# The first modulation of a hybrid encoder layer: weight blocks stationary, two or four columns of c moving

## The chip, the cores and the metric

The kernel runs on one NeuronCore of a Trainium2 chip. The core has TensorE (PE in the profile; its weight loads are listed apart as PEld), VectorE (DVE), ScalarE (ACT), GpSimd (POOL) and SyncE (SP), which here only issues transfers, and 16 DMA engines. The metric is the device time of one execution in microseconds, as the median of several. The chip can grant TensorE less than its full clock; the profile lists the granted clock (1.00 is full).

## The reference

One encoder layer for 512 prompt frames and 64 sample frames, with D = 2048. What matters here is its first step: a vector c per request (one for the prompt, one for the sample) goes through SiLU and a matrix of 2048 x 12288, which gives six modulation vectors; the first two shift and scale the normalised input before the big input projection.

```
mod = jax.nn.silu(c) @ w_ada[l] + b_ada[l]
sh1, sc1, g1, sh2, sc2, g2 = jnp.split(mod[:, None, :], N_MOD, axis=-1)
h = rmsnorm(x, norm1[l]) * (1 + sc1) + sh1
mix, s_a, s_b, s_c = token_mixers(h, ...)      # begins with proj = h @ w_in
x = x + g1 * mix
h = rmsnorm(x, norm2[l]) * (1 + sc2) + sh2
f, s_f = conv_ffn(h, ...)
x = x + g2 * f
```

All inputs and outputs are float32.

## The kernel before

After the opening stage (`head`) come the head recurrences with the rest of the input projection, the output projection, the up projection with its convolution, and the down projection. All large products are made from float32r parts: a float32 operand is split into a rounded high part and a remainder (`split`: ScalarE makes `wh`, L649; VectorE makes `wl` as the difference, L650), and three products of parts replace one float32 product (`mm6`, L561 and L563).

`head` computes the vectors sh1 and sc1 (indices 0 and 1 of `mod`) in four groups g of 512 columns. `modulation(g)` does for each group two halves, first the scale (mi = 1), then the shift (mi = 0). A half reads eight weight tiles from `w_ada`, each of 256 rows by 512 columns in 512 KB, as two blocks of 128 rows (k). Six of the eight are split into `wh` and `wl`. The other two (k0 = 4 and 12) stay whole in float32; over the eight halves these are sixteen tiles. The tiles land in `hraw` (5 buffers) or `raw` (3 buffers); split parts have three buffers each.

On TensorE the columns of c are the stationary operand and the weights move, 512 columns at a time, into one PSUM bank. For split tiles the stationary operand is `cst[:, k]` with NW = 66 columns, of which four hold something (the high parts and the remainders of the two vectors) and the rest are zeros written by GpSimd; there are four such matmuls per tile (L757, L758). For whole tiles it is `cs4[:, k]` with four columns, two of them zeros, in float32 (L753, two per tile). The result lies in four PSUM rows, 512 columns wide. It is brought onto the partitions in three steps: VectorE copies it to `rw` (L760), four small matmuls of `rw` against a selection matrix add high part and remainder and turn it (L763, into a second bank `pc`), and VectorE adds the bias b_ada into `mod` (`put_mod`, L797). After both halves `scale_mod` (L803) makes the scale `s1`.

With group 0's modulation the input x is loaded, transposed on TensorE (L698) and its row sums made (L725, L726); the vectors (biases, gains) are loaded and transposed (L623, L624). From there on the order is: modulation(g + 1), then for the four k of group g the split of the modulated x (`split_mod`, L583, L584, L586: `tmp`, `hh`, `hl`), the narrow columns (L877) and two blocks of the projection (L561, L563; the groups of the profile with `fh`, `fl`). What is called here "products" are those 256 matmuls of 288 moving columns.

A scheduler decides the order on each engine from the order of the code and priorities: loads and splits of weight tiles are issued with a raised priority (`high_priority`), so they stand some instructions earlier than in the code. Each engine works through its own queue in that order.

The same helper pattern appears later, in `ada_block` (L820, L826): there the other four modulation vectors are made by VectorE, and sixteen matmul instructions per block (L826: `acc`, 128 x 128, stationary, one column of ones moving) sum them over partitions.

Of the kernel before, what the change touches and what calls it, by code (L numbers as in the profile page):

```python
# [8 lines left out]
F32 = mybir.dt.float32  # L9
F32R = mybir.dt.float32r  # L10
I32 = mybir.dt.int32
AF = mybir.ActivationFunctionType
ALU = mybir.AluOpType
# [3 lines left out]
P = 128  # L17
D = 2048
KD = 16
# [28 lines left out]
NW = 66  # L48
# [53 lines left out]
class Kern:  # L102
# [554 lines left out]
    def head(self, pool):  # L657
        nc, i = self.nc, self.i
        V, A, T = nc.vector, nc.scalar, nc.tensor
# [2 lines left out]
            next(vectors)  # L662

        self.ct = self.cp.tile([P, 2, KD], F32, name="ct")
        cst = pool.tile([P, KD, NW], F32R, tag="cst", bufs=1, name="cst")
        nc.gpsimd.memset(cst.bitcast(F32), 0.0)
        for s in range(2):
            A.activation(self.ct[:, s], self.vmap[f"c{s}"], AF.Silu)
        cs4 = pool.tile([P, KD, 4], F32, tag="cs4", bufs=1, name="cs4")
        nc.gpsimd.memset(cs4, 0.0)  # L670
        for s in range(2):
            V.tensor_copy(cs4[:, :, s], self.ct[:, s])
            A.activation(cst[:, :, s], self.ct[:, s], AF.Copy)
            V.tensor_tensor(cst[:, :, 2 + s], self.ct[:, s], cst[:, :, s].bitcast(F32), op=ALU.subtract)
        self.mod = self.cp.tile([P, 6, KD, 2], F32, name="mod")
# [61 lines left out]
        def hraw():  # L737
            if next(turns) == "r":
                return self.raw()
            return pool.tile([P, 1024], F32, tag="hraw", bufs=5, name=self.name("hraw"))  # L740

        def modulation(g, between=lambda: None):
            for mi in (1, 0):
                ps = self.bank()
                c0 = mi * D + g * 512
                for k0 in range(0, KD, 2):
                    between()
                    src = i["w_ada"][0, k0 * P:(k0 + 2) * P, c0:c0 + 512].rearrange("(k p) n -> p k n", p=P)
                    if k0 in (4, 12):
                        raw = hraw().rearrange("p (k n) -> p k n", k=2)  # L750
                        nc.sync.dma_start(raw, src)
                        for k in range(2):
                            T.matmul(ps[:4], cs4[:, k0 + k], raw[:, k], start=False, stop=False)  # L753
                        continue
                    wh, wl = self.wtile(src, hraw())
                    for k in range(2):
                        T.matmul(ps[:NW], cst[:, k0 + k], wh[:, k], start=(k0 + k == 0), stop=False)  # L757
                        T.matmul(ps[:NW], cst[:, k0 + k], wl[:, k], start=False, stop=(k0 + k == KD - 1))  # L758
                rw = pool.tile([4, 512], F32, tag="rw", bufs=1, name=self.name("rw"))
                V.tensor_copy(rw, ps[:4])  # L760
                pc = self.bank()
                for j in range(4):
                    T.matmul(pc[:, 2 * j:2 * j + 2], rw[:, j * P:(j + 1) * P], self.c["sel"][:4, 16:18], start=True, stop=True)  # L763
                self.put_mod(mi, 4 * g, pc)
                for _ in vectors:
                    pass
            self.scale_mod(s1, 1, "norm1", 4 * g)

        plan = [[] for _ in range(16)]
        for b in range(5):  # L770
            for f, at in ((x_load, 0), (x_turn, X_LAG), (x_norm, X_LAG + 1)):
                plan[X_AT[b] + at].append(lambda f=f, b=b: f(b))
        step = iter(plan)
        modulation(0, lambda: [f() for f in next(step)])
        rx = x_rows()
        self.ps_nar, self.ps_q0 = self.pgt(), self.pgt()
        for g in range(4):
            if g < 3:
                modulation(g + 1)
            ks = range(4 * g, 4 * g + 4)  # L780
            nar = self.narrow_w(pool, 4 * g)
            qw, kw = [self.split(pool, self.w_in(off)(4 * g, 4 * g + 4), "f", 512, 3) for off in (OFF_BQ, OFF_BK)]
            for k in ks:
                hh, hl = self.htiles(k)
                tmp = pool.tile([P, 2, HT], F32, tag="tmp", bufs=2, name=self.name("tmp"))
                self.split_mod(xT[:, k], rx, s1[:, k], self.mod[:, 0, k], hh, hl, tmp)
                nc.sync.dma_start(self.xs[k], xT[:, k])
                self.h.append((hh, hl))
                self.mm_narrow(k, nar[:, k % 4])
                for ps, w in ((self.ps_q0, qw), (ps_k0, kw)):  # L790
                    self.mm6(ps, w[0][:, k % 4], w[1][:, k % 4], self.h[k], k == 0, k == KD - 1)
        raw = self.xr()
        self.ps_k0 = raw[:, :2 * HT].rearrange("p (h t) -> p h t", h=2)
        V.tensor_copy(self.ps_k0, ps_k0[:, :, :HT])

    def put_mod(self, mi, k0, pc):
        self.nc.vector.tensor_tensor(  # L797
            self.mod[:, mi, k0:k0 + 4], pc[:, :8].rearrange("p (j s) -> p j s", s=2),
            self.vec("b_ada", mi * KD + k0, 4).unsqueeze(2).to_broadcast([P, 4, 2]), op=ALU.add)

    def scale_mod(self, out, mi, norm, k0, n=4):

# [1188 lines left out]
```

## Time and profile before

| | |
|---|---|
| Median of 3 runs | 2870.66 us (2866.38 to 2871.43) |
| The profiled execution | 2869.18 us |
| Its span, first to last instruction | 2867.4 us |
| Mean granted TensorE clock | 0.992 |
| PE busy | 2810.4 us (98%), 20596 matmul instructions |
| PEld busy | 2708.7 us (94%) |
| DVE busy | 2301.9 us (80%) |
| ACT busy | 1355.0 us (47%) |
| POOL busy | 320.6 us (11%) |
| HBM read, written | 356.24 MB, 40.13 MB |

In the page's rows a group reads: line, engine, operation, result <- operands (buffer numbers left out), for a matmul the stationary block as rows*columns and the result, the count, then busy time, mean duration in ns, and the idle time of the engine just before with what ended it. Matmuls overlap and their ends are modelled, so the time between two starts in the timeline says more of their cost than their durations. Times in the timeline and the windows are us from the span's start. The opening stage takes the first 160 us.

### The profile page before, as it was taken

How to read it: one execution, taken by the hardware profiler on the slowest of the kernel's cores; microseconds unless marked ns; L12 is line 12 of the kernel's file. 1: busy time of each engine (PE TensorE's matmuls, PEld its weight loads, DVE VectorE, ACT ScalarE, POOL GpSimd, SP SyncE). 2: the span in 40 equal slices, each digit the busy share in tenths (PEclk: the TensorE clock that was granted, in tenths of full speed). 3: DMA queues.
4: the chain of work that ended last, by engine and by line, in shares of the span. 5: the costliest groups of instructions: out<-in, count | busy, mean ns of one | idle time of the engine just before them, and what ended most of it. 6: DMA issues, size and time to landing. Idle time of an engine off the chain costs nothing.

```text
span 2867.4 us, 52042 instructions
## 1 busy us (share of the span) xinstructions
PE 2810.4 (98%) x20596; PEld 2708.7 (94%) x20596; DVE 2301.9 (80%) x3742; ACT 1355.0 (47%) x2379; POOL 320.6 (11%) x587
## 2 busy tenths in 40 slices
PE   7999999999999999999999999999999999999998
PEld 3599999999999999999999999999999999999997
DVE  5788878777778777468888888888887889999995
ACT  7574566544333333255444444444444464434453
POOL 0005432224310001001000000000000000000000
PEclk9999999999999999999999999999999999999999
DMA  9975555545455448433333333333333343443451
GB/s 308 306 209 148 157 149 161 158 140 152 129 166 172 146 131 251 123 119 102 102 101 102 108 106 108 102 108 108 101 101 105 105 150 114 123 127 118 126 169 67
DMA packets 522441, 399.80 MB, mean 139 GB/s; under 512 B 50793, under 2 KB 453956, under 8 KB 522196
## 3 DMA queue, kind: packets, MB, share of 16 engines
q1 hardware_dynamic: 516772, 385.79, 45.3%
q0 software_dynamic: 5424, 10.68, 1.2%
q8 instruction: 162, 2.65, 0.4%
q14 instruction: 83, 0.68, 0.1%
HBM read 356.24 MB, written 40.13 MB: 138 GB/s over the span
## 4 chain that ended last, share of the span: by engine, by line
PE 82%; DVE 9%; DMA 3%; ACT 3%; issue 2%; SPq 0%; POOL 0%; ACTq 0%; DVEq 0%
PE g L561 19%; PE g L563 10%; PE g L1373 9%; PE g L1374 8%; PE g L1375 8%; PE bank L1374 3%; PE bank L1373 3%; PE bank L1375 3%; DVE wl L1558 2%; PE g L1606 2%; PE g L1608 2%; PE g L1607 2%; DMA raw<-in_w_down_dram 1%; PE bank L162 1%; PE bank L826 1%
## 5 line engine op out<-in xcount | busy, mean ns | idle before, releaser
L1373 PE MATMUL g<-slot,wh 128*128 128x290 f32 x1760 | 534.2, 304 | 2.4 <-ACT p L1385 2.4
L1374 PE MATMUL g<-slot,wh 128*128 128x290 f32 x1760 | 526.6, 299 | 0.0
L1375 PE MATMUL g<-slot,wl 128*128 128x290 f32 x1760 | 520.9, 296 | 0.0
L561 PE MATMUL g<-hh,wh 128*128 128x288 f32 x1984 | 450.4, 307 | 2.4 <-ACT hh L1160 1.3
L561 PE MATMUL g<-hl,wh 128*128 128x288 f32 x1984 | 432.3, 298 | 0.0
L563 PE MATMUL g<-hh,wl 128*128 128x288 f32 x1984 | 432.0, 298 | 0.0
L1320 ACT ACTIVATE wh<-raw 128x1024 fp32r<-128x1024 f32 x176 | 186.8, 1061 | 393.1 <-PE g L1374 376.8
L1373 PEld LDWEIGHTS g<-slot,wh 128*128 128x128 f32 x1760 | 331.8, 189 | 16.9 <-ACT p L1385 11.3
L1375 PEld LDWEIGHTS g<-slot,wl 128*128 128x128 f32 x1760 | 337.2, 192 | 0.0
L1374 PEld LDWEIGHTS g<-slot,wh 128*128 128x128 f32 x1760 | 335.6, 191 | 0.1
L561 PEld LDWEIGHTS g<-hh,wh 128*128 128x128 f32 x1984 | 319.1, 190 | 5.6 <-ACT hh L1160 1.5
L561 PEld LDWEIGHTS g<-hl,wh 128*128 128x128 f32 x1984 | 321.3, 189 | 0.3
L563 PEld LDWEIGHTS g<-hh,wl 128*128 128x128 f32 x1984 | 319.6, 189 | 0.2 <-issue 0.2
L649 ACT ACTIVATE wh<-raw 128x1024 fp32r<-128x1024 f32 x163 | 172.6, 1059 | 309.1 <-PE g L561 272.6
L650 DVE TENSOR_TENSOR wl<-raw,wh 128x1024 fp32r<-128x1024 f32 x163 | 199.1, 1222 | 52.8 <-ACT wh L649 50.9
L820 DVE SCALAR_TENSOR_TENSOR acc<-xr,ct,acc 128x512 f32<-128x512 f32 x322 | 230.4, 751 | 1.5 <-DMA xr<-in_w_ada_dram 1.5
L1321 DVE TENSOR_TENSOR wl<-raw,wh 128x1024 fp32r<-128x1024 f32 x176 | 214.8, 1220 | 19.3 <-ACT wh L1320 19.2
L1606 PE MATMUL g<-slot,wh 128*128 128x288 f32 x760 | 224.8, 296 | 2.3 <-DVE slot L1623 1.1
L1608 PE MATMUL g<-slot,wl 128*128 128x288 f32 x760 | 224.4, 296 | 0.3 <-DVE wl L1558 0.3
L1607 PE MATMUL g<-slot,wh 128*128 128x288 f32 x760 | 224.4, 295 | 0.0
L1374 PE MATMUL bank<-slot,wh 128*128 128x290 f32 x704 | 210.3, 299 | 0.0
L1373 PE MATMUL bank<-slot,wh 128*128 128x290 f32 x704 | 209.6, 298 | 0.0
(416 smaller groups left out, 6083.0 us busy)
## 6 DMA issues: line engine op xcount, KB each, us to landing
raw<-in_w_up_dram SPq DMA_DIRECT2D x176, 512.0 KB, 4.0
raw<-in_w_in_dram SPq DMA_DIRECT2D x108, 512.0 KB, 3.9
xr<-in_w_ada_dram SPq DMA_DIRECT2D x86, 512.0 KB, 3.9
raw<-in_w_down_dram SPq DMA_DIRECT2D x76, 512.0 KB, 3.6
ax<-in_w_ada_dram SPq DMA_DIRECT2D x42, 512.0 KB, 3.7
hraw<-in_w_ada_dram SPq DMA_DIRECT2D x40, 512.0 KB, 9.5
raw<-in_w_out_dram SPq DMA_DIRECT2D x32, 512.0 KB, 4.3
raw<-in_w_ada_dram SPq DMA_DIRECT2D x24, 512.0 KB
```

What stands on the lines that cost most here:

```text
L561: T.matmul(ps[:, h if bank is None else bank, :n], wh, x[:, h, :n], start=f, stop=False)
L563: T.matmul(ps[:, h if bank is None else bank, :n], wl, ah[:, h, :n], start=False, stop=stop)
L650: nc.vector.tensor_tensor(lo[:, :n_], raw[:, :n_], hi[:, :n_].bitcast(F32), op=ALU.subtract)
L820: V.scalar_tensor_tensor(acc[s], w[:, k], col, acc[s], op0=ALU.mult, op1=ALU.add)
L1320: self.nc.scalar.activation(hi, src, AF.Copy)
L1321: self.nc.vector.tensor_tensor(lo, src, hi.bitcast(F32), op=ALU.subtract)
L1373: T.matmul(ps, wh[:, j], hi, start=(c < 3 and j == 0), stop=False, skip_group_check=True)
L1374: T.matmul(ps, wh[:, j], lo, start=False, stop=False, skip_group_check=True)
L1375: T.matmul(ps, wl[:, j], hi, start=False, stop=(j == NPAIR - 1), skip_group_check=True)
L1606: T.matmul(ps, wh[:, j, f], hi, start=(c < 3 and j == 0), stop=False, skip_group_check=True)
L1607: T.matmul(ps, wh[:, j, f], lo, start=False, stop=False, skip_group_check=True)
L1608: T.matmul(ps, wl[:, j, f], hi, start=False, stop=(j == n - 1), skip_group_check=True)
```

## The change

The operands of the modulation's matmuls change places. Now a block of 128 x 128 weights is stationary, four blocks (j) to the 512 columns of a tile, and columns of c move: `cst[:, k]`, now four columns wide without padding, against each block of `wh` and of `wl`; and `ct[:, :, k]`, the two vectors in float32, against each block of a whole tile. The result lies on the partitions at once: 16 columns of the bank, for each j two sums x (with the high parts of c and with the remainders) for two vectors s; the whole tiles add to the first two of each four. The turn through `rw`, the selection matrix and `pc` goes; VectorE adds bias and high sums into a small `rw`, then the remainder sums into `mod`. `cs4`, its copies and both zero fills go. The sixteen whole tiles stay whole. Nothing else in the code is edited; line numbers behind the change move by a few.

```diff
-        cst = pool.tile([P, KD, NW], F32R, tag="cst", bufs=1, name="cst")
-        nc.gpsimd.memset(cst.bitcast(F32), 0.0)
+        cst = pool.tile([P, KD, 4], F32R, tag="cst", bufs=1, name="cst")
...
-        cs4 = pool.tile([P, KD, 4], F32, tag="cs4", bufs=1, name="cs4")
-        nc.gpsimd.memset(cs4, 0.0)
         for s in range(2):
-            V.tensor_copy(cs4[:, :, s], self.ct[:, s])
             A.activation(cst[:, :, s], self.ct[:, s], AF.Copy)
             V.tensor_tensor(cst[:, :, 2 + s], self.ct[:, s], cst[:, :, s].bitcast(F32), op=ALU.subtract)
...
-                ps = self.bank()
+                ps, n = self.bank(), 0
...
                         for k in range(2):
-                            T.matmul(ps[:4], cs4[:, k0 + k], raw[:, k], start=False, stop=False)
+                            for j in range(4):
+                                T.matmul(ps[:, 4 * j:4 * j + 2], raw[:, k, j * P:(j + 1) * P], self.ct[:, :, k0 + k],
+                                         start=False, stop=False, skip_group_check=True)
                         continue
-                    wh, wl = self.wtile(src, hraw())
-                    for k in range(2):
-                        T.matmul(ps[:NW], cst[:, k0 + k], wh[:, k], start=(k0 + k == 0), stop=False)
-                        T.matmul(ps[:NW], cst[:, k0 + k], wl[:, k], start=False, stop=(k0 + k == KD - 1))
-                rw = pool.tile([4, 512], F32, tag="rw", bufs=1, name=self.name("rw"))
-                V.tensor_copy(rw, ps[:4])
-                pc = self.bank()
-                for j in range(4):
-                    T.matmul(pc[:, 2 * j:2 * j + 2], rw[:, j * P:(j + 1) * P], self.c["sel"][:4, 16:18], start=True, stop=True)
-                self.put_mod(mi, 4 * g, pc)
+                    for w in self.wtile(src, hraw()):
+                        for k in range(2):
+                            for j in range(4):
+                                T.matmul(ps[:, 4 * j:4 * j + 4], w[:, k, j * P:(j + 1) * P], cst[:, k0 + k],
+                                         start=n == 0, stop=n == 12 * KD // 2 - 1, skip_group_check=True)
+                                n += 1
+                two = ps[:, :16].rearrange("p (j x s) -> p j x s", j=4, x=2)
+                rw = pool.tile([P, 4, 2], F32, tag="rw", bufs=2, name=self.name("rw"))
+                V.tensor_tensor(rw, two[:, :, 0], self.mod_bias(mi, 4 * g), op=ALU.add)
+                V.tensor_tensor(self.mod[:, mi, 4 * g:4 * g + 4], two[:, :, 1], rw, op=ALU.add)
```

In the changed kernel L757 and L758 have become L756, L753 has become L750, L760 and L797 (for this use) L761 and L762.

The instructions move at these places. TensorE around the end of group 0's modulation and the start of group 1's, before (`bank` is the PSUM tile of a half):

```order
L757 MATMUL bank_427<-wh_589,cst 66x512
L758 MATMUL bank_427<-wl_590,cst 66x512
L763 MATMUL bank_600<-consts_95,rw_598 128x2 x4
L757 MATMUL bank_621<-wh_623,cst 66x512
L758 MATMUL bank_621<-wl_624,cst 66x512
```

The same place on TensorE now:

```order
L750 MATMUL bank_501<-ct,hraw_724 128x2 x8
L756 MATMUL bank_501<-cst,wh_735 128x4 x8
L756 MATMUL bank_501<-cst,wl_736 128x4 x8
L756 MATMUL bank_774<-cst,wh_776 128x4 x8
L756 MATMUL bank_774<-cst,wl_777 128x4 x8
```

The four matmuls on `rw` between the halves are gone, and a tile's matmuls on `wh` now all stand ahead of those on `wl`.

TensorE at the end of group 2's second half before, where the products of group 1 (`hh`/`hl` against `fh`/`fl`) begin:

```order
L757 MATMUL bank_976<-wh_1036,cst 66x512
L758 MATMUL bank_976<-wl_1037,cst 66x512
L561 MATMUL g_620<-hh_1073,fh_1062 128x288 x2
L561 MATMUL g_620<-hl_1074,fh_1062 128x288 x2
L563 MATMUL g_620<-hh_1073,fl_1063 128x288 x2
```

The same place on TensorE now:

```order
L756 MATMUL bank_1366<-cst,wl_1467 128x4 x8
L561 MATMUL g_773<-hh_1542,fh_1531 128x288 x2
L561 MATMUL g_773<-hl_1543,fh_1531 128x288 x2
L750 MATMUL bank_1366<-ct,hraw_1487 128x2 x8
L756 MATMUL bank_1366<-cst,wh_1498 128x4 x8
L756 MATMUL bank_1366<-cst,wl_1499 128x4 x8
L563 MATMUL g_773<-hh_1542,fl_1532 128x288 x2
```

Four of the products have moved ahead of the half's last two tiles.

VectorE at the end of group 0's second half, before (`wl` is the low part of a weight tile, `hl` that of the modulated x):

```order
L650 TENSOR_TENSOR wl_624<-hraw_622,wh_623 128x1024
L760 COPY rw_598<-bank_427 4x512
L650 TENSOR_TENSOR wl_634<-hraw_632,wh_633 128x1024
L797 TENSOR_TENSOR mod<-bank_600,cols 128x8
L650 TENSOR_TENSOR wl_648<-hraw_646,wh_647 128x1024
```

The same place on VectorE now:

```order
L650 TENSOR_TENSOR wl_736<-raw_734,wh_735 128x1024
L761 TENSOR_TENSOR rw_756<-bank_501,cols 128x8
L762 TENSOR_TENSOR mod<-bank_501,rw_756 128x8
L586 SCALAR_TENSOR_TENSOR hl_1107<-tmp_1108,mod,hh_1106 128x2x256
L650 TENSOR_TENSOR wl_777<-hraw_775,wh_776 128x1024
```

The split of the next half's first tile (`wl_624` before, `wl_777` now) stood ahead of the instruction that reads the finished bank, and stands behind it now.

More of the change, by code (lines that the diff above doesn't have):

```diff
@@ L794, in head, with mod_bias @@
         V.tensor_copy(self.ps_k0, ps_k0[:, :, :HT])
+    def mod_bias(self, mi, k0):
+        return self.vec("b_ada", mi * KD + k0, 4).unsqueeze(2).to_broadcast([P, 4, 2])
     def put_mod(self, mi, k0, pc):
-        self.nc.vector.tensor_tensor(
-            self.mod[:, mi, k0:k0 + 4], pc[:, :8].rearrange("p (j s) -> p j s", s=2),
-            self.vec("b_ada", mi * KD + k0, 4).unsqueeze(2).to_broadcast([P, 4, 2]), op=ALU.add)
+        self.nc.vector.tensor_tensor(self.mod[:, mi, k0:k0 + 4], pc[:, :8].rearrange("p (j s) -> p j s", s=2),
+                                     self.mod_bias(mi, k0), op=ALU.add)
     def scale_mod(self, out, mi, norm, k0, n=4):
```

## The prediction

> **What bounds the kernel now.** I read the page's slices first, then the windows of the opening stage, then its groups and its timeline. The slices (busy tenths, granted TensorE clock in tenths, DMA share in tenths, 71.7 us each):
>
> ```profile
> PE   7999999999999999999999999999999999999998
> PEclk9999999999999999999999999999999999999999
> DMA  9975555545455448433333333333333343443451
> ```
>
> TensorE is busy from the second slice to the last at nearly the full clock, so what lengthens TensorE's work lengthens the kernel, unless TensorE waits there. Only in the first two slices is DMA as busy, and there the changed code lies. I cut them where the first modulation matmul starts (11.2), where group 0's modulation ends (57.2) and where the last product of the stage ends (159.7); the columns are busy time with the count of instructions, clock, DMA share and GB/s:
>
> ```profile
> core 0: us, PE busy (x) PEld busy (x) DVE busy (x) ACT busy (x) POOL busy (x), PEclk, DMA share, GB/s
> 11.20:57.20 46.00, 38.43 (x161) 19.95 (x161) 19.25 (x40) 34.40 (x74) 2.75 (x5) 0.85 0.92 311
> 57.20:159.70 102.50, 99.53 (x504) 62.33 (x504) 81.96 (x126) 57.93 (x84) 1.15 (x3) 1.00 0.92 302
> ```
>
> Stage 1 (11.2 to 57.2) has 7.6 us of idle TensorE; stage 2 has 3.0 of 102.5. TensorE bounds stage 2, with DMA close behind at 0.92. VectorE has 20 us to spare there and ScalarE 45.
>
> **What is removed.** Groups of 0 to 160 us (count, busy, mean ns, idle before):
>
> ```profile
> L757 PE MATMUL bank<-wh,cst 128*66 128x512 f32 x96 | 40.9, 426 | 0.5 <-DVE cst L674 0.5
> L758 PE MATMUL bank<-wl,cst 128*66 128x512 f32 x96 | 39.9, 415 | 0.6 <-DVE wl L650 0.6
> L753 PE MATMUL bank<-raw,cs 128*4 128x512 f32 x32 | 15.6, 610 | 0.0
> L763 PE MATMUL bank<-consts,rw 4*128 4x2 f32 x64 | 8.4, 249 | 4.9 <-DVE rw L760 4.9
> L561 PE MATMUL ps_k<-hh,fh 128*128 128x288 f32 x32 | 6.9, 296 | 0.0
> ```
>
> L753 has a second group, as large, from `hraw`. A mean here contains the modelled end, which overlaps the next matmul. The pace is read from starts, in the timeline (start, duration):
>
> ```profile
> 69.18 1.05 PE L763 MATMUL bank<-consts,rw 4*128 4x2 f32 x8 [0.78 <-DVE rw L760]
> 70.16 0.45 PE L757 MATMUL bank<-wh,cst 128*66 128x512 f32 x1
> 70.44 0.40 PE L758 MATMUL bank<-wl,cst 128*66 128x512 f32 x1
> ...
> 71.83 0.40 PE L758 MATMUL bank<-wl,cst 128*66 128x512 f32 x1
> 72.16 1.88 PE L753 MATMUL bank<-raw,cs 128*4 128x512 f32 x4
> 73.97 0.44 PE L757 MATMUL bank<-wh,cst 128*66 128x512 f32 x1
> ...
> 149.14 0.43 PE L877 MATMUL g<-hh,nar 128*66 128x288 f32 x2
> ...
> 157.59 0.43 PE L877 MATMUL g<-hh,nar 128*66 128x288 f32 x2
> ```
>
> From 70.44 to 71.83 are six starts: 0.232 us per float32r matmul of 512 columns. A whole float32 tile takes 1.81 us. The eight L763 take 0.98 us (69.18 to 70.16). Modulation in all: 192 x 0.232 + 16 x 1.81 + 8 x 0.98 + 4.9 waited for `rw` = 44.5 + 29.0 + 7.8 + 4.9 = 86 us. Between 149.14 and 157.59 are 64 products of 288 columns, 0.132 us each; there are eight groups of 32 like the L561 row, so 256 x 0.132 = 33.8 us that remain.
>
> **What is added.** A split tile becomes 16 matmuls whose stationary block has 128 columns and which move only 4; a whole tile becomes 8 float32 matmuls. A float32 matmul is two instructions in the trace (four for the two of a tile at 72.16), a float32r one is one. Per half-modulation that is 6 x 16 + 2 x 16 = 128 loads of 128 columns, 1024 in all. What such a pair costs shows in L826, later, where a 128x128 block meets a single column:
>
> ```profile
> 408.21 1.84 PE L826 MATMUL bank<-consts,acc 128*128 128x1 f32 x16
> 409.92 0.52 PE L561 MATMUL g<-hl,wh 128*128 128x288 f32 x2
> ...
> 412.03 0.68 PE L563 MATMUL g<-hh,wl 128*128 128x288 f32 x2
> 412.51 0.68 PE L561 MATMUL g<-hh,wh 128*128 128x288 f32 x2
> ...
> 528.33 1.84 PE L826 MATMUL bank<-consts,acc 128*128 128x1 f32 x16
> 530.03 0.76 PE L561 MATMUL g<-hh,wh 128*128 128x288 f32 x2
> ```
>
> Sixteen pairs take 1.71 and 1.70 us: 0.107 us each, the load and not the column. A float32r load of 128 columns lasts as long as a float32 one in the groups (188 ns, below, against L763's 186), so I take 0.107 for both. At that price a half-modulation is 13.7 us, where 10.8 (86/8) stood.
>
> **The clock then doubles it.** The windows around those two stretches:
>
> ```profile
> 407.20:410.60 3.40, 3.22 (x28) 2.99 (x27) 1.05 (x5) 2.37 (x6) 0.00 (x0) 1.00 0.04 10
> 410.60:414.10 3.50, 3.50 (x17) 3.50 (x16) 3.50 (x7) 0.78 (x2) 0.67 (x1) 0.51 0.24 38
> 526.70:530.10 3.40, 3.40 (x34) 3.33 (x31) 1.54 (x3) 3.05 (x7) 2.93 (x7) 1.00 0.43 126
> 530.10:533.50 3.40, 3.40 (x16) 3.40 (x16) 3.29 (x7) 1.56 (x2) 2.85 (x8) 0.50 0.00 0
> ```
>
> TensorE was never idle for long before either drop (3.22 and 3.40 of 3.40 busy; loads 2.99 and 3.33), and yet the grant fell to half right after 16 weight-bound pairs. So weight loads don't hold the clock up; moving columns do. Of the 16 such stretches in the program two dropped it: one of them, 1.7 us, is only half as long as the 3.4 us that the grant then stayed down. The new stretches last 13 us and more with 4 columns per pair, and the matmuls between them are few, as the order shows. [...]
>
> What a load costs at half clock no stream here shows. Loads of 128 columns at full clock (groups, first row), at half in a stream (410.7 to 414), and alone at half:
>
> ```profile
> L563 PEld LDWEIGHTS ps_k<-hh,fl 128*128 128x128 f32 x32 | 5.3, 188 | 0.2 <-DVE fl L650 0.2
> ...
> L561 PEld LDWEIGHTS g<-hh,wh 128*128 128x128 f32 x6 | 1.6, 319 | 0.0
> ...
> 1315.79 0.29 PEld L1373 LDWEIGHTS g<-slot,wh 128*128 128x128 f32 x1 [2.33 <-ACT p L1385]
> ```
>
> Alone it grows from 0.188 to 0.29, by 0.10, which is one more 0.107: the load runs at the granted clock, 0.213 us. Bounds: 0.107 (not slowed) and 0.240 (products of 288 columns at half clock, 412.03 to 412.51, whose loads keep up). I take 0.213. [...]
>
> The order shown with the change has nothing between the halves any more: the turn through `rw` is gone with its 4.9 us of waits, and long rows of small matmuls follow each other. Where products come, they come in a block; the four (0.5 us) that moved ahead of the last 24 small matmuls of a half are too few to raise the clock.
>
> **A wait that is new.** On VectorE (the last place shown with the change) the next half's first split, `wl`, stood ahead of the instruction that waits for the half's last matmul; now it is queued behind it. ScalarE's split of that tile stands behind `hh` in the same way. Durations, groups of stage 2:
>
> ```profile
> L650 DVE TENSOR_TENSOR wl<-hraw,wh 128x1024 fp32r<-128x1024 f32 x23 | 28.0, 1219 | 3.5 <-ACT wh L649 3.4
> L586 DVE SCALAR_TENSOR_TENSOR hl<-tmp,mod,hh 128x512 fp32r<-128x512 f32 x16 | 12.0, 747 | 1.8 <-ACT hh L584 1.8
> L797 DVE TENSOR_TENSOR mod<-bank,cols 128x8 f32<-128x8 f32 x7 | 1.1, 164 | 4.1 <-PE bank L763 4.0
> ...
> L649 ACT ACTIVATE wh<-hraw 128x1024 fp32r<-128x1024 f32 x22 | 23.1, 1053 | 8.7 <-PE bank L757 4.3 <-DMA hraw<-in_w_ada_dram 4.0 <-PE bank L753 0.3
> L584 ACT ACTIVATE hh<-tmp,mod 128x512 fp32r<-128x512 f32 x16 | 11.5, 718 | 16.0 <-DVE tmp L583 8.1 <-DVE mod L797 7.8
> ```
>
> At this place TensorE waits 2 x 0.16 + 0.72 + 1.05 = 2.1 us. Inside a group three small adds, one 0.75 us multiply and the split, 2.5 us, lie against eight pairs on `wh`, 1.7 us: 0.8 us. At the other three group ends products cover part; I take 1 each. Together 2.1 + 3 x 1 + 4 x 0.8 = 8 us, 1 of it in stage 1.
>
> **The sum.** The transposes, which stay:
>
> ```profile
> L698 PE MATMUL g<-consts,hs 128*128 128x128 f32 x64 | 9.1, 281 | 1.6 <-ACT xT L701 1.6
> L698 PE MATMUL g<-consts,hs 64*128 64x64 f32 x16 | 2.2, 318 | 0.0
> ```
>
> Stage 1: 256 x 0.213 = 54.5; transposes, row sums and vectors 12 (11.3 us busy and some 4 of smaller ones, less overlapping ends); 2 of the 7.6 idle is left, 1 for the new wait. 69.5 for 46.0: +23.5. Stage 2: 768 x 0.213 = 163.6; products 33.8; restarts 3; the new wait 7; about 7 because three blocks of products start cold (half clock for 3.4 to 6.8 us, say 5, each losing 5 x (1 - 0.132/0.240) = 2.3); less about 9 because after two blocks the full clock lasts on for some 4.5 us. 205.4 for 102.5: +102.9. Together +126 on the profiled 2869.18 (span 2867.4; the median is 2870.66, 0.05% off): **2995 us**. With 0.240 per load it is +27.6, 3023.
>
> The other edits I cost at nothing. The four copies and memsets of `cst`/`cs` go; they lay ahead of the first matmul, which waited 0.5 us for `cst`. The transfers keep their number, and a slower TensorE only gives them time.
>
> **Rivals.** The clock stays full (0.06): 16 loads then were not the cause of the drops. Stage 1 needs 256 x 0.107 + 15 = 42, still under DMA's 46; stage 2 82.2 + 33.8 + 3 + 7 = 126: +23.5, 2893. Against it stand both drops.
>
> The clock falls, loads stay at 0.107 (0.05): +23.5 + 7, 2900; against it the 0.29.
>
> Faster (0.03): float32r loads hide. Deciding point: stage 2 breaks even at (102.5 - 43.8)/768 = 76 ns a pair. A transpose's load of the same 128 columns is shorter,
>
> ```profile
> L698 PEld LDWEIGHTS g<-consts,hs 128*128 128x128 f32 x64 | 7.2, 142 | 4.0 <-ACT xT L701 2.8 <-issue 0.4
> ```
>
> 46 ns less than 188; at 107 - 46 = 61 ns and full clock stage 2 is 46.8 + 33.8 + 10 = 90.6, 12 less, of which DMA at 0.92 leaves 8: 2861. Against it: the float32r loads here last 188.
>
> No effect (0.02), 2869: data, not TensorE, bounds stage 2; its 3.0 idle of 102.5 speaks against.
>
> **Chances and range.** The forecast has 0.84; its own range runs from 2955 (the clock up more often than I count) to 3025 (0.240 per load), and holds 0.80 of the 0.84, so it is the whole range; the next cases lie 55 us and more below it. Under 0.2% a measurement can't tell: faster 0.03, same 0.02, slower 0.95.
>
> **What will tell.** Windows inside long rows of L756 should show clock 0.50 and about 16 loads per 3.4 us; the last L877 should start near 283 us, not 157.6; DMA share in the opening falls near half; after it the timeline is the old one, shifted. Clock 1.00 there, or pairs at 0.107, would prove me wrong.

## The result and the profile after

The changed kernel takes **3005.63 us** (median of 4, 3000.87 to 3008.13) against 2869.55 for the kernel before (median of 4): 1.0475 times, 95% interval 1.0459 to 1.049, slower. The forecast was 2995 us in a range of 2955 to 3025, slower with 0.95. The profiled execution took 3000.87 us with a span of 2999.1, 131.7 longer than the span before.

The page's slices of the kernel after (75 us each):

```profile
PE   7999999999999999999999999999999999999998
PEclk8556999999999999999999999999999999999999
DMA  6445555545644555743333333333333343443461
```

TensorE is as busy as before, and the DMA share of the first slices fell from 9 to 6 and 4. The loss stands in one row: 8, 5, 5 and 6 tenths of the clock in the first four slices, where all slices were 9. The 8 flatters the first slice: the profile has no grant from before 40.0 us and the row counts that time as full clock, but eight pairs (a pair is a weight load with its matmul) take 1.71 us there too (12.80 to 14.51), as at half clock below.

Windows of the kernel after, one through each of the long rows of L756 and one in the last block of products:

```profile
core 0: us, PE busy (x) PEld busy (x) DVE busy (x) ACT busy (x) POOL busy (x), PEclk, DMA share, GB/s
57.20:91.30 34.10, 32.94 (x151) 30.76 (x151) 8.32 (x17) 7.31 (x17) 0.54 (x1) 0.50 0.36 109
93.60:120.00 26.40, 26.40 (x124) 26.40 (x125) 11.33 (x16) 10.41 (x15) 0.00 (x0) 0.50 0.44 140
166.30:220.00 53.70, 51.97 (x242) 51.88 (x242) 15.65 (x27) 11.64 (x16) 0.00 (x0) 0.50 0.44 144
231.20:282.40 51.20, 49.47 (x230) 49.38 (x230) 14.31 (x24) 11.08 (x15) 0.00 (x0) 0.50 0.39 120
282.40:296.80 14.40, 14.40 (x108) 14.10 (x107) 7.07 (x13) 6.56 (x13) 0.00 (x0) 1.00 0.77 214
```

TensorE is 100% busy from 93.6 to 120 and has half the clock all the same; DMA, at 0.92 of the old stage, is at 0.4. In these rows the full clock comes back with the products (last row) and not with the small matmuls.

TensorE's timeline of the kernel after (start, duration, what, the wait ahead of it):

```profile
84.44 3.55 PE L750 MATMUL bank<-ct,hraw 128*128 128x2 f32 x16
87.85 1.85 PE L756 MATMUL bank<-cst,wh 128*128 128x4 f32 x8
89.56 1.85 PE L756 MATMUL bank<-cst,wl 128*128 128x4 f32 x8
93.56 1.87 PE L756 MATMUL bank<-cst,wh 128*128 128x4 f32 x8 [2.16 <-ACT wh L649]
...
162.72 1.03 PE L756 MATMUL bank<-cst,wl 128*128 128x4 f32 x8
163.61 1.03 PE L756 MATMUL bank<-cst,wh 128*128 128x4 f32 x8
164.50 1.03 PE L756 MATMUL bank<-cst,wl 128*128 128x4 f32 x8
165.40 2.73 PE L750 MATMUL bank<-ct,raw 128*128 128x2 f32 x16
167.99 1.84 PE L756 MATMUL bank<-cst,wh 128*128 128x4 f32 x8
```

Eight pairs take 1.71 us in the first rows (87.85 to 89.56): 0.213 us each. For a short time after a block of products they take 0.89 us (163.61 to 164.50), 0.111 each, until the clock falls at 166.3. Group 0's modulation ends at 91.3, where it ended at 57.2, and the last product at 296.8, where it was 159.7. Stage 1 is 34.1 us longer, stage 2 103.0; behind them this execution runs as before, and a few microseconds faster.

### The profile page after: what moved, and what is told of

Read it like the earlier page. It is cut to its first block, busy times and chain, and to the rows that moved or that the text cites. A ratio compares the mean times of both kernels' runs of the same rounds, so it can differ in the third digit from the quotient of the medians.

```text
span 2999.1 us, 53437 instructions
## 1 busy us (share of the span) xinstructions
PE 2942.2 (98%) x21300; PEld 2891.3 (96%) x21300; DVE 2298.0 (77%) x3740; ACT 1355.1 (45%) x2379; POOL 320.7 (11%) x585
## 4 chain that ended last, share of the span: by engine, by line
PE 81%; DVE 5%; ACT 2%; DMA 2%; issue 1%; POOL 0%; SPq 0%; ACTq 0%; DVEq 0%; POOLq 0%
PE g L561 18%; PE g L563 9%; PE g L1373 8%; PE g L1374 8%; PE g L1375 8%; PE bank L1374 3%; PE bank L1373 3%; PE g L1608 3%; PE g L1606 3%; PE bank L1375 3%; PE g L1607 3%; PE bank L1608 1%; DVE acc L820 1%; PE bank L1606 1%; PE bank L1607 1%
## 5 line engine op out<-in xcount | busy, mean ns | idle before, releaser
L1321 DVE TENSOR_TENSOR wl<-raw,wh 128x1024 fp32r<-128x1024 f32 x176 | 214.5, 1219 | 19.8 <-ACT wh L1320 19.6
```

The costliest lines, as they stand in the source:

```text
L1321: self.nc.vector.tensor_tensor(lo, src, hi.bitcast(F32), op=ALU.subtract)
```

## The experiments

Times are medians beside the kernel before on the same chip (2867.5 to 2869.3 us in the comparisons).

### no_wl: is it the loads that set the time?

```
-                    for w in self.wtile(src, hraw()):
+                    wh, wl = self.wtile(src, hraw())
...
-                                T.matmul(ps[:, 4 * j:4 * j + 4], w[:, k, j * P:(j + 1) * P], cst[:, k0 + k],
+                                T.matmul(ps[:, 4 * j:4 * j + 4], wh[:, k, j * P:(j + 1) * P], cst[:, k0 + k],
```

The products with the low parts `wl` are left out; `wl` is still made.

> The changed kernel without the matmuls on the low parts of the weights in the first modulation (left out: 384 of the 1024 loads; the splits are still made, so the result lacks that part). If the opening is bound by the loads at half clock, the time falls by 384 x 0.213 = 82 us, to about 2923. If something else sets the pace (splits on VectorE and ScalarE, transfers), it falls by much less.

Measured: 2921.69 us (one run), 83.9 less than the changed kernel. 384 pairs at 0.213 are 82. So the time follows the weight loads at the price of the half clock; transfers and splits, which all remained, don't set the pace.

### wide128, wide96, wide64: what holds the clock?

The same 1024 loads, with more columns moved through each block. The added columns are the neighbours of the wanted ones in `cst` and zeros behind them; their results are not read. For 128 (float32 tiles have half as many, since a float32 matmul is two instructions in the trace: 16 of L750 for the eight of a tile):

```
-        cst = pool.tile([P, KD, 4], F32R, tag="cst", bufs=1, name="cst")
+        cw = pool.tile([P, KD * 4 + 128], F32R, tag="cst", bufs=1, name="cst")
...
-                                T.matmul(ps[:, 4 * j:4 * j + 4], w[:, k, j * P:(j + 1) * P], cst[:, k0 + k],
+                                T.matmul(ps[:, 128 * j:128 * j + 128], w[:, k, j * P:(j + 1) * P], cw[:, 4 * (k0 + k):4 * (k0 + k) + 128],
```

> The changed kernel, but each matmul of the modulation moves 128 columns where it moved 4 (64 where it moved 2 in float32): the columns that count come first, the others are those of the next blocks of c or zeros, and their results are not read. The loads are the same 1024. Theory 1 (moving columns hold the clock, loads don't, and a load goes at the granted clock): 128 columns last 53 ns at full clock and hide under a load of 107, but keep the array about half busy, so the clock stays at 1.00 in the opening, a pair takes 0.107 to 0.112 us, stage 2 about 128 us instead of 203, stage 1 about 50; 2895 to 2910 us in all. Theory 2 (a load of 128 columns next to a tiny product is slow by itself and the half clock only goes along with it): more columns can't help, 3005 or more.

> The same with 96 columns (48 in float32): 40 ns of streaming per load of 107, 0.37 of the time. Theory 1 with the threshold between the 3.4 us windows of the kernel before that kept the clock (0.34 and up by my count of columns) and those that lost it (0.28): clock stays up, within 10 us of the variant with 128. If the threshold lies above 0.4: as the changed kernel, about 3005.

> The same with 64 columns (32 in float32): 27 ns of streaming per load of 107, 0.25 of the time. Theory 1: below what kept the clock, so the grant falls to 0.50 in the rows of small matmuls and the time is that of the changed kernel, 2995 to 3010. If any streaming is enough: 2895 to 2910.

The 53, 40 and 27 ns for the columns are an estimate: 512 columns take 0.427 us at the pace of half clock (kernel before, starts from 11.74 to 14.30 us), and half of that is taken for full clock. The 0.232 us measured at full clock would make them 58, 44 and 29.

Measured: wide128 **2917.03 us** (ratio 1.0163, 1.0146 to 1.018), 88.6 less than with 4 columns; wide96 2975.56 and wide64 2986.05 (one run each). Thirty-two times the columns make the kernel faster: the first theory, that moving columns hold the grant and loads don't, stands, though its band is missed by 7 us. wide96 and wide64 lost the clock and are below the times forecast for that, for two reasons. In stage 1 they had the full clock for 24 and 10 us, up to about 50 us, where the changed kernel had it for 7. And the scheduler ordered VectorE otherwise in them: the next tile's `wl` stands ahead of the two adds again, and the new wait is gone. wide64, groups of 0 to 300 us:

```profile
L761 PE MATMUL bank<-cst,wl 128*128 128x64 f32 x384 | 87.3, 390 | 0.0
```

From the first narrow product to the last (138.5 to 277.6 us), wide64 takes 3.1 us less than the changed kernel (152.8 to 294.9) and has 3.5 us of waits fewer, with the same two stretches of 10.2 us at full clock before the last block: there the new wait is worth about its length. Windows of wide128:

```profile
46.00:74.40 28.40, 26.82 (x233) 25.37 (x232) 14.78 (x26) 16.72 (x32) 0.54 (x1) 1.00 0.83 252
74.40:115.40 41.00, 39.11 (x182) 39.09 (x183) 19.45 (x30) 14.12 (x18) 0.00 (x0) 0.50 0.85 278
122.20:149.50 27.30, 27.30 (x248) 27.30 (x246) 12.61 (x17) 10.77 (x12) 0.00 (x0) 1.00 0.62 193
```

and of wide96, a block of products and the row of pairs behind it:

```profile
128.10:134.80 6.70, 6.70 (x52) 6.70 (x52) 4.79 (x12) 2.54 (x7) 0.32 (x1) 1.00 1.01 343
138.30:186.00 47.70, 47.70 (x226) 47.70 (x225) 15.68 (x19) 12.25 (x13) 0.00 (x0) 0.50 0.60 184
```

With 96 columns the clock falls 3.5 us after the products (134.8 to 138.3), with 4 it fell after 4.4 and 5.4 (161.9 to 166.3 and 225.8 to 231.2). With 128 it holds through rows of pairs (third row of wide128), 248 pairs in 27.3 us, 0.110 each, where a pair with 4 columns took 0.111. But the middle row is a surprise: between 74.4 and 115.4 us the same rows of the same kernel ran at half for 41 us. Just ahead of it stands a wait, in wide128's timeline:

```profile
71.95 1.11 PE L761 MATMUL bank<-cst,wl 128*128 128x128 f32 x8 [0.70 <-DVE wl L650]
72.89 1.06 PE L761 MATMUL bank<-cst,wh 128*128 128x128 f32 x8
76.29 1.97 PE L761 MATMUL bank<-cst,wl 128*128 128x128 f32 x8 [2.34 <-DVE wl L650]
```

So it looked as if a wait could knock the clock down, and as if 128 columns could hold a full clock but not win it back. The next two runs were to take the waits away.

### late_put and wide_late: the waits taken away, or so it was meant

Each half's two adds (and `scale_mod`) are issued three tiles later in the code; late_put is the changed kernel with that, wide_late the one with 128 columns.

```
+                    if k0 == 6:
+                        put_held()
...
+                def put(mi=mi, ps=ps):
+                    two = ps[:, :16].rearrange("p (j x s) -> p j x s", j=4, x=2)
...
+                held.append(put)
+                if g == 0 and mi == 1:
+                    put_held()
```

> Theory (the waits at the ends of the halves are real time on TensorE's path): the changed kernel's waits for the next tile's wh and wl after a half, 8.3 us in its timeline, go when the half's two adds are issued three tiles later: 2996 to 2999 us against 3005.6. Rival (the time is set by the loads and the waits only move, for instance to the data or to the products): 3003 to 3008 us. Both expect the clock at half in the rows of the small matmuls.

> 128 moving columns (the extra ones are not read) and the adds issued three tiles later. Theory (128 columns hold the full clock, and a wait of some 2 us of TensorE is what drops it): the clock stays near full from the first products on, pairs 0.11 us, 2885 to 2897 us: then the flip itself, at full clock, costs 16 to 28 us over the kernel before. Rival (the clock falls for some other reason, waits or none): 2912 to 2920 us as with 128 columns and the adds in their place.

Measured: 3006.14 us (3003.02 to 3010.26) and 2919.68 us (2919.18 to 2924.78): no difference from the kernels without the edit. The waits in the groups of 0 to 300 us of late_put,

```profile
L764 PE MATMUL bank<-cst,wl 128*128 128x4 f32 x384 | 84.9, 343 | 4.4 <-DVE wl L650 4.4
L764 PE MATMUL bank<-cst,wh 128*128 128x4 f32 x384 | 84.4, 342 | 3.5 <-ACT wh L649 2.2 <-DVE cst L670 1.3
```

and of the changed kernel,

```profile
L756 PE MATMUL bank<-cst,wl 128*128 128x4 f32 x384 | 85.4, 344 | 4.4 <-DVE wl L650 4.4
L756 PE MATMUL bank<-cst,wh 128*128 128x4 f32 x384 | 85.2, 343 | 3.7 <-ACT wh L649 2.2 <-DVE cst L670 1.6
```

are the same, because the order is. VectorE's queue at the end of group 0 in late_put:

```
L650 TENSOR_TENSOR wl_704<-raw_702,wh_703 128x1024
L650 TENSOR_TENSOR wl_736<-raw_734,wh_735 128x1024
L770 TENSOR_TENSOR rw_825<-bank_501,cols 128x8
L771 TENSOR_TENSOR mod<-bank_501,rw_825 128x8
L586 SCALAR_TENSOR_TENSOR hl_1103<-tmp_1104,mod,hh_1102 128x2x256
```

The adds stand behind the same two `wl` as without the edit. Issuing an instruction later in the code doesn't move it here; the scheduler put it back. Neither run tested what its expectation says; what wide64 shows of the new wait, above, is the nearest that the runs have.

### whole_only: one part of the change alone

The kernel before, with only the sixteen whole float32 tiles flipped. They sum into the bank `pc`, and the turn of `rw` adds to it.

```
-                            T.matmul(ps[:4], cs4[:, k0 + k], raw[:, k], start=False, stop=False)
+                            for j in range(4):
+                                T.matmul(pc[:, 2 * j:2 * j + 2], raw[:, k, j * P:(j + 1) * P], self.ct[:, :, k0 + k],
+                                         start=n == 0, stop=False, skip_group_check=True)
+                                n += 1
```

> The kernel before with only the whole float32 tiles flipped: 16 weight loads of 128 columns with 2 moving columns, in place of 4 instructions of 512 columns, between the rows of float32r matmuls that stream 512 columns. Theory (weight loads lower the clock only where they last about a whole window; a tile of 1.7 us between streaming matmuls does not): clock 1.00 in nearly all windows of the stage, 1.71 to 1.79 us for a tile where 1.81 stood, 2866 to 2872 us, no change that can be measured. Rival (any such row drops the clock for 3.4 us and more): 16 rows lose 1.7 us and more each, 2890 us and above.

Measured: **2910.43 us** (2899.99 to 2917.41), ratio 1.0146 (1.0123 to 1.0169). The theory falls: 256 loads, in rows of 1.71 us between rows of 512 columns, cost 42.7 us, though the tiles themselves became no longer. From the first modulation matmul to the last product the stage has 102 us at half clock where 14 stood, and TensorE waits 22.8 us where it waited 10.5; the scheduler also ordered TensorE and VectorE otherwise than before. What each of these costs is not separated here. Windows of its stage, at the steps of the grant (3.41 us each, as long as the half clock of the kernel before from 410.6 and from 530.1 us), show how the clock falls:

```profile
73.20:76.50 3.30, 3.30 (x9) 1.89 (x8) 1.88 (x3) 1.63 (x2) 0.00 (x0) 0.50 0.93 289
76.60:79.90 3.30, 2.54 (x20) 1.96 (x18) 0.72 (x2) 1.35 (x2) 0.00 (x0) 1.00 0.49 179
80.00:83.30 3.30, 3.30 (x12) 2.67 (x13) 2.41 (x5) 0.02 (x1) 0.00 (x0) 0.50 0.00 0
83.40:86.70 3.30, 3.25 (x8) 1.47 (x7) 3.30 (x5) 2.00 (x2) 0.00 (x0) 0.50 0.00 0
86.80:90.10 3.30, 3.30 (x24) 2.72 (x23) 2.89 (x4) 1.06 (x1) 0.00 (x0) 1.00 0.00 0
90.20:93.50 3.30, 1.00 (x5) 0.33 (x3) 0.69 (x1) 0.63 (x1) 0.00 (x0) 1.00 1.04 284
```

and its timeline:

```profile
73.13 0.63 PE L761 MATMUL bank<-wl,cst 128*66 128x512 f32 x1
...
76.11 0.59 PE L760 MATMUL bank<-wh,cst 128*66 128x512 f32 x1
76.54 1.85 PE L754 MATMUL bank<-ct,hraw 128*128 128x2 f32 x16
78.25 0.42 PE L761 MATMUL bank<-wl,cst 128*66 128x512 f32 x1
```

From 73.13 to 76.11 seven matmuls of 512 columns start, 0.426 us each: at half clock a column takes 0.83 ns, at full clock half of that by the grant, 0.416 (the measured pace, 0.232 us for 512 columns, is 0.453, so a full row comes to 0.91 by this estimate). With this the share of a window in which columns move can be worked out from all the starts in it (columns by 0.83 or 0.416 ns; a float32 instruction twice that, since the four of a whole tile of the kernel before take 1.81 us, 0.453 each, against 0.232), and set beside what the grant was in the window behind. The shares in this table are such estimates:

| window of (start, us) | granted | share with columns moving | granted next |
|---|---|---|---|
| whole_only, 76.5 (one flipped tile, a wait) | 1.0 | 0.20 | 0.5 |
| whole_only, 86.8 (one flipped tile, no wait) | 1.0 | 0.46 | 1.0 |
| whole_only, 90.2 (a wait of 2.6 us) | 1.0 | 0.23 | 0.5 |
| whole_only, 131.1 | 1.0 | 0.37 | 0.5 |
| whole_only, 66.3 | 0.5 | 0.68 | 0.5 |
| whole_only, 73.1 | 0.5 | 1.00 | 1.0 |
| whole_only, 83.4 | 0.5 | 0.91 | 1.0 |
| before, 55.7 (its lowest behind 50 us) | 1.0 | 0.40 | 1.0 |
| wide128, 71.0 (a wait of 0.70 us and the first 0.46 of that of 2.34) | 1.0 | 0.25 | 0.5 |
| wide128, ten windows from 78 to 112 | 0.5 | 0.50 | 0.5 |
| wide128, 122 to 150 and 160 to 187 | 1.0 | 0.47 to 0.52 | 1.0 |
| wide96, 134.9 and 196.3 | 1.0 | 0.36 | 0.5 |

Two limits, not one. The same estimate over the opening (from 50 us on) of all the kernels traced here gives: the full grant was kept in every window with 0.40 or more and lost in every one with 0.38 or less; at half clock it came back in every window above 0.77, in some of those at 0.75 to 0.77, and in none below but one (0.44, at 50.3 us of the kernel after, where transposes run; the last section returns to it). By this estimate a wait and a weight load count alike: nothing moves. The flipped tile at 86.8 did no harm with streaming on both sides, the one at 76.5 did with 0.8 us of idling in its window.

### wide_fill: more work, less time?

If so, filling the wait of wide128 with moving columns must keep its clock up. Ten matmuls of 512 columns, into a bank that nobody reads, stand at the place of the 2.34 us wait:

```
+                        if (g, mi, k0, x) == (1, 1, 10, 1):
+                            fill = self.bank()
+                            for m in range(10):
+                                T.matmul(fill[:4], cst[:, m], first[:, m % 2], start=True, stop=True, skip_group_check=True)
```

> The kernel with 128 moving columns and, where TensorE waited 2.34 us for wl in group 1, ten float32r matmuls of 512 columns into a bank that nobody reads (2.3 us of work added; the rows after it are unchanged). Theory (the grant falls when too few columns move in a 3.4 us window, below some 0.4 of it, and comes back only above some 0.75; 128 columns per pair give about 0.5, which holds the full clock and can't bring it back): the clock stays 1.00 from about 44 to past 115 us, the 41 us at half are gone, and the kernel with more work is faster, 2893 to 2903 us against 2917. Rival (the fall at 74 us has another cause, for instance the row of pairs itself): 2914 to 2922 us.

Measured: 2911.6 us (2909.96 to 2915.18), ratio 1.0154 (1.0139 to 1.017), against 1.0163 (1.0146 to 1.018) without: the medians stand 5.4 us apart, in the direction of the theory, but outside both bands of the expectation, and the intervals overlap. The clock did what the theory says, and up to 205 us of wide128 all its instructions on TensorE and VectorE stand in the same order in wide_fill, with only the fill between them. Windows of wide_fill:

```profile
44.90:70.00 25.10, 24.76 (x219) 23.60 (x218) 11.10 (x17) 14.90 (x29) 0.54 (x1) 1.00 0.79 256
70.00:96.00 26.00, 24.25 (x205) 22.60 (x204) 16.82 (x29) 12.01 (x17) 0.00 (x0) 1.00 1.02 330
96.00:106.20 10.20, 3.92 (x17) 3.90 (x18) 5.80 (x7) 4.11 (x5) 0.00 (x0) 0.50 0.73 215
```

Full clock through 74.4, where wide128 lost it for 41 us, until 96. There the gain went, into a wait that the slow clock had hidden (timelines of TensorE and ScalarE):

```profile
94.02 1.09 PE L767 MATMUL bank<-cst,wh 128*128 128x128 f32 x8
102.28 1.97 PE L767 MATMUL bank<-cst,wl 128*128 128x128 f32 x8 [7.17 <-DVE wl L650]
...
99.74 0.63 ACT L649 ACTIVATE fh<-raw 128x512 fp32r<-128x512 f32 x1 [10.68 <-DMA raw<-in_w_in_dram]
```

The DMA share is 1.02 there: TensorE has caught up with the transfers, `wl` is queued behind a split that waits for one, and TensorE stands for 7.2 us. That wait then costs the clock, for 10 us more. The stage has a second bound close behind the first, as it had before the change.

### whole_wide: the same tile with 64 columns

whole_only with 64 float32 columns moving through each block in place of 2 (62 of them not read).

```
-                                T.matmul(pc[:, 2 * j:2 * j + 2], raw[:, k, j * P:(j + 1) * P], self.ct[:, :, k0 + k],
+                                T.matmul(pc[:, 64 * j:64 * j + 64], raw[:, k, j * P:(j + 1) * P], ck[:, 4 * (k0 + k):4 * (k0 + k) + 64],
```

> The kernel with only the whole tiles flipped, their 2 moving columns widened to 64 float32 ones (the extra ones are not read): the same 16 loads per tile, the same order. Theory (the columns that move decide): clock back to about 0.99, 1.75 to 1.8 us per tile, 2864 to 2880 us. Rival (a row of weight loads lowers the clock whatever moves): 2900 to 2918 us, as with 2 columns.

Measured: 2890.47 us (2889.79 to 2892.92), ratio 1.0082 (1.0065 to 1.0099): 20 us of whole_only's 43 are gone, by columns that nobody reads. The band of the theory was missed by 10 us and the rival's by 10 as well. The expectation takes the order to be the same; in the two traces TensorE and VectorE are ordered differently. TensorE's waits in the stage still come to much the same (20.5 us, 22.8 in whole_only), while the time at half clock went from 102 to 58 us, so the gain goes with the clock. Windows that held with 64 columns (whole_only lost the clock at the tile of 76.5 us):

```profile
69.60:89.90 20.30, 16.22 (x104) 11.89 (x103) 15.51 (x24) 10.10 (x14) 0.00 (x0) 1.00 0.64 201
90.00:100.20 10.20, 10.20 (x43) 9.53 (x43) 6.82 (x13) 5.59 (x10) 0.00 (x0) 0.50 1.04 388
```

By the same estimate the windows with most of a widened tile in them and no long wait kept the grant, at 0.42 to 0.72; the drops that remain (0.13 to 0.38, the one at 90.0 behind a wait of 2.39 us for a transfer) have waits in them. A wide tile has little to spare for a wait.

### wide112: the limit, forecast

> 112 moving columns (56 in float32; the extra ones are not read) where 128 and 96 were run. The columns take 112/2.4 = 47 ns of the 112 ns of a pair at full clock: 0.42 of a window. Theory (estimate from the windows of the other runs: the full grant is kept at 0.39 of a window and above and lost at 0.38 and below): the clock holds in the rows of pairs after the first products, as with 128 columns, and the time is 2905 to 2930 us. Rival (the limit lies between 112 and 128, or there is none and the time falls evenly with the columns, 2976 at 96 and 2917 at 128): the clock falls inside the rows as with 96 columns, 2945 to 2980 us.

The 2.4 there are columns per ns, from the estimate of 0.416 ns for a column (0.83 at half clock in whole_only, halved).

The edit is that of wide128 with 112 and 56 columns. Measured: 2935.44 us (one run), 5 us above the theory's band and 10 below the rival's. Windows of wide112:

```profile
42.60:49.40 6.80, 5.40 (x49) 5.16 (x49) 2.90 (x5) 6.44 (x14) 0.54 (x1) 1.00 1.01 363
49.40:131.30 81.90, 81.90 (x381) 80.01 (x381) 34.88 (x55) 26.56 (x40) 0.00 (x0) 0.50 0.70 208
138.20:165.40 27.20, 27.20 (x246) 27.20 (x246) 15.15 (x19) 13.07 (x14) 0.00 (x0) 1.00 0.68 206
175.70:199.50 23.80, 23.80 (x216) 23.80 (x215) 13.96 (x18) 10.01 (x11) 0.00 (x0) 1.00 0.45 136
```

The mechanism is as forecast: behind the first products the clock holds through two rows of pairs, 51 us, at an estimated 0.41 to 0.43. The time is longer since an earlier wait, at 46 to 49 us (1.4 us of idling in the first row, a share of 0.27, with transposes among the pairs), had put the clock down, and rows at half clock with 0.44 then left it down for 82 us without one idle moment (81.90 busy of 81.90). Both limits show in one kernel: 0.42 keeps the clock in the last two rows, and 0.44 doesn't bring it back in the second.

### before_late: a version that might beat both

The kernel before, with the copy to `rw` issued two tiles later and the turn and `put_mod` four tiles later, against its 4.9 us of waits for `rw`.

```
+                    if k0 in (4, 8) and held:
+                        held.pop(0)()
...
-                V.tensor_copy(rw, ps[:4])
+                held.append(lambda rw=rw, ps=ps: V.tensor_copy(rw, ps[:4]))
```

> The kernel before with each half's copy out of the bank issued two tiles later and its turn four tiles later. Theory (TensorE's 4.9 us of waits for rw are on the path of the stage): 2864 to 2867 us, 0.1 to 0.2 per cent less. Rival (data sets the pace of the stage, DMA share 0.92 there): within 2 us of the kernel before.

Measured: 2873.06 us (11 runs) against 2867.72 (15): ratio 1.0018 (1.0009 to 1.0027), a little slower; neither expectation held. The waits for `rw` have shrunk, and others have come, in the groups of 0 to 167 us of before_late:

```profile
L766 PE MATMUL bank<-wl,cst 128*66 128x512 f32 x96 | 40.3, 420 | 6.9 <-DVE wl L650 6.8
...
L773 PE MATMUL bank<-consts,rw 4*128 4x2 f32 x64 | 8.4, 249 | 1.8 <-DVE rw L768 1.8
```

Waits for `rw` went from 4.9 to 1.8 us, those for `wl` from 0.6 to 6.9. Whether the new order of VectorE or the data behind it makes `wl` late stays open. No version run here beats the kernel before.

## Why the prediction was right, step by step

**The clock.** Right, and the cause is shown: with the same 1024 loads, in rows of pairs without an idle moment behind a block of products, the moving columns decide whether the full clock stays (lost with 4, 64 and 96, kept with 112 and 128). The orders of these kernels differ elsewhere, but not within such rows. The reading of the two old drops, that 16 pairs can drop the clock, was right; in whole_only such a row did it at 155.0 us with 0.14 us of waiting beside it.

**0.213 us per pair at half clock.** Right (87.85 to 89.56); the bounds 0.107 and 0.240 weren't needed. At full clock it is 0.111.

Idle time was not needed for the half clock here: 26.4 us of TensorE busy without a gap (93.6 to 120) ran at 0.50, and windows of 3.41 us with up to 0.38 of moving columns by the estimate above, not idle ones, were enough to fall.

**Stage 2, 205.4 us.** It took 205.5 (91.3 to 296.8). From start to start the pairs take 155.0 (163.6 - 9 = 154.6 in the forecast), the products 42.1 (33.8 + 7 = 40.8) and the waits 8.4 (7 + 3 = 10). The 7 and the 9 were estimates. The kernel before shows half clock for 3.41 us (from 410.6 and 530.1) and for 6.83 (from 1315.2), but nothing in it shows the 4.5 us for which the full clock was to outlast a block; in the kernel after three blocks began with 4.9, 5.7 and 4.2 us at half clock (from 151.2, 215.2 and 278.2), and the full clock outlasted two by 4.4 and 5.4 (from 161.9 and 225.8). Each term is near; that the sum meets to a tenth is luck, since the misses cancel. The new wait was 8 us by the forecast, 7 of it here, and is 8.3 in the timeline, but not where it was forecast: 2.16 at the end of group 0 (2.1 forecast), then 0.94, 1.73 and 1.74 for `wl` inside groups (0.8 each forecast), and 1.73 for a split of the products at one of the three later group ends (1 at each forecast).

**Stage 1, 69.5 us.** This is the step that failed: it took 80.2 (11.1 to 91.3). The pairs' 54.5 is right (54.4). The term "transposes, row sums and vectors 12" was mis-sized, since it was taken at the pace of the full clock. Groups and timeline of the kernel after:

```profile
L694 PE MATMUL g<-consts,hs 128*128 128x128 f32 x64 | 15.2, 406 | 1.7 <-ACT xT L697 1.7
L623 PE MATMUL bank<-consts,hs 88*128 88x88 f32 x3 | 1.1, 353 | 4.0 <-DVE cols L624 4.0
...
17.92 4.01 PE L694 MATMUL g<-consts,hs 128*128 128x128 f32 x16
21.73 3.41 PE L750 MATMUL bank<-ct,raw 128*128 128x2 f32 x16
```

Sixteen transposes take 3.81 us, 0.238 each; their group is 15.2 us busy where it was 9.1. From start to start all transposes of x take 16.2, the matmuls of the row sums (L721, L722) 2.6 and the vectors (L623) 1.0: 19.8 in all for the term of 12. The idle time left was 2 in the forecast and is 6.0: 4.0 of L623, which waits for VectorE's copies, queued behind row sums that wait for the late transposes, 1.7 of the transposes (L694) and 0.3 of L721. The 1.6 waited for `cst` lies ahead of 11.1, outside the stage. The 1 us of new wait didn't come in this stage. With 54.4 for the pairs that is the 80.2.

**The sum.** Both stages together are 137.1 us longer, 11 more than forecast. Of that 5.8 came back later: matmuls that are the same in both kernels start 138.1 us later at 172 us of the old timeline and 132.3 later at its end. They come closer in steps. Two, of 1.5 and 1.4 us, lie at the clock's short drops of the kernel before (410 and 530 us), against which the kernel after has one elsewhere (422); the others (1.3 at 810 us, 0.9 from 1020 to 1090, 2.1 from 2360 to 2410) lie where both have the full clock, and their cause stays open. So 3000.9 for this execution and 2995 forecast: a miss of 10.7 in a stage, half covered by something that was not forecast. That cover is luck of one execution: the medians lie 136.1 apart, 10 more than the 126 forecast, about the miss of stage 1.

**The rivals.** Full clock throughout: the pairs would have had to run at 0.111 everywhere; they did for 4 us behind a block. Load not slowed: refuted by 0.213. Loads that hide: refuted by 0.111 a pair at full clock, above the 0.076 at which stage 2 breaks even. Data that bounds the stage: refuted by a DMA share of 0.4. What the last rival pointed to is there all the same, one step behind: with the clock held up, wide_fill ran into the transfers.

**What was to tell.** Clock 0.50 in L756's rows, 16 loads per 3.4 us, the timeline later shifted, but for the 5.8 us: as written. The L877 that started at 157.6 starts at 294.5 where 283 was forecast (stage 1's miss).

## What to carry to other kernels

A busy TensorE row said nothing about its clock here (100% busy from 93.6 to 120 us at a grant of 0.50): count the moving columns. The form of the product that trades moving columns for weight loads paid twice, for each load (0.111 us a pair at full clock) and then for the half clock (0.213), and it passed that on to its neighbours (the transposes, 15.2 us busy where they were 9.1). Where a scheduler orders the queues, look at the order after an edit before measuring it: an instruction issued later may stand where it stood (late_put), and an edit that leaves the order alone in the code may change it on the engines (wide64, whole_wide).

## What the runs showed of the hardware that was not expected

- The grant showed two limits, by the estimate above: from 50 us on it was kept at 0.40 of a window with columns moving, lost at 0.38, and regained only from about 0.75. Rows in between kept whichever clock they found: 51 us at full and 82 us at half in one kernel (wide112).
- Therefore 1.2 to 1.4 us of waiting within one window could cost 41 us of half clock (wide128) and 82 (wide112), and 2.3 us of work put into the wait took the 41 away.
- Unread columns bought time: 88.6 us (wide128) and 20.0 us (whole_wide), though the order on the engines changed along with them.
- Up to about 50 us, where transposes run among the pairs, the estimate doesn't fit if a transpose counts with its 128 columns: wide96 kept the full grant from 32 to 49 us at 0.21 to 0.35. Counted twice, as the other float32 instructions are, it fits there too. Over the openings of all thirteen traces the lowest window that kept the full grant then has 0.40 and the highest that lost it 0.39 (wide96, 49.5 us); the odd window at 50.3 us of the kernel after has 0.90. One window stays out of line: 0.91 at 59.1 us of wide64 did not bring the clock back (0.50 from 49 to 140 us). This is an estimate from starts, and no run was made to test it.
